# Two of the modulation's column blocks summed on VectorE instead of multiplied on TensorE

## The chip, the cores and the metric

The kernel runs on one core of a Trainium2 chip. The metric is the time of one execution in microseconds, taken on the device; for the kernel before the median of three runs is 1099.94 us. Beside the time there is one profile of one execution, with every instruction of every engine: TensorE (PE, and PEld for its weight loads), VectorE (DVE), ScalarE (ACT), GpSimd (POOL) and SyncE (SP), whose queue issues most of the DMAs of this kernel.

## The reference, cut to what matters

The program is one decoder layer on a sequence of 1024 tokens of width 1024 in float32. Ahead of everything stands a modulation: a vector c goes through silu and a 1024 x 6144 matrix, and its first two parts, shift and scale, change the normalised input. What the change touches is this:

```
c_act = jax.nn.silu(c)
mod = c_act @ w_ada[l] + b_ada[l]
sh1, sc1, g1, sh2, sc2, g2 = [m[:, None, :] for m in jnp.split(mod, N_MOD, axis=-1)]
h = rmsnorm(x, pre_w_mix[l]) * (1.0 + sc1) + sh1
proj = h @ w_in[l]
aq, ak, av, hq, hf, hi, hg = jnp.split(proj, _SPLITS, axis=-1)
```

Behind it follow windowed attention on aq, ak, av, a gated recurrence on the rest, an output projection, a second modulation and a squared-ReLU MLP. None of that is touched.

## The kernel before

**Tiles.** The 1024 columns of h are eight blocks of 128 (kb = 0 to 7), the tokens two halves of 512. For each block and half, x is transposed on TensorE (`first_T`), so that a column of h lies on a partition, and shift and scale of the block are one number per partition. `split_evac` (line 224) then makes two tiles of 128x512: ScalarE writes `hhi` (scaled and shifted, rounded to the matmul's type), GpSimd forms `f` from it, VectorE writes the rest, `hlo`. Each product with a weight is three passes on TensorE: high by high, high by low, low by high. The weights are split the same way: ScalarE copies the high part (`first_wq`, `first_kv`), VectorE subtracts to get the low part (`first_wql`, tiles `wq1l`, `wkv1l` and so on).

**The loop of the first stage** (lines 406 to 455) goes over kb for the first half of the tokens and adds into open PSUM banks for q (`pq`) and for k and v (`pk`). In one turn, TensorE does: the high products of block kb for four groups of 128 tokens (`first_mm(..., 0)`), the fold of a modulation if there is one, the transposes of x for block kb + 1, and the low products of block kb (`first_mm(kb, tb, 1)`). The evacuation of a block needs its shift (`sh1`), its scale (`a1`) and, on GpSimd, the negated shift (`ns1`). From line 336 to line 640 each of ScalarE, VectorE, GpSimd and TensorE executes in exactly the order in which the program is written (`pin`); behind line 640 the framework orders the instructions by a plan of its own.

**The modulation.** Shift and scale of blocks 0 and 1 come one block at a time. Blocks 2 and 3, 4 and 5, 6 and 7 come in pairs, as q = (1, 0), (2, 0), (3, 0). For a pair, eight tiles of weights (128x512 each, `wa`) hold the 1024 rows of c by 256 columns of shift (gate 0) and 256 of scale (gate 1), two blocks of rows side by side in a tile. `mod_mm` (line 281) multiplies them on TensorE: 16 products of 128x256 for the first half of kp and 16 for the second, with c spread over 32 columns as the stationary side, so that four sets run in four column groups. `mod_copy` brings the result to SBUF, and `mod_fold` turns it with two products against a constant, adds the bias on VectorE and writes `sh1`, `a1` and `ns1`. The table `nextq` says in which turn each pair is made: pair (2, 0) in turn kb = 3, its first reader being the evacuation of block 4, pair (3, 0) in turn kb = 5, for block 6.

**Loads.** SyncE's queue issues, in this order: x for the first half, `wa` of blocks 0 and 1, a first weight, `wa` of pair (1, 0), weights, `wa` of pair (2, 0), weights, `wa` of pair (3, 0), weights. Within a pair the tiles come as kp = 0, 1, 2, 3, each with gate 0 and then gate 1. In turn kb = 3 the loads of x for the second half are issued; ScalarE squares them in turns 5 and 6 (`norm_sq`, tiles `jx`), VectorE scales them in turns 6 and 7. The tiles `f`, `jx`, the copy of `mod_copy` and the sums of later modulations share one pool of five places (`t_`).

Later modulations (`modacc`, line 146) are already summed on VectorE, with tiles named `macc`; the later stage from 180 us on shows these operations.

Of the kernel before, what the change touches and what calls it, by code (L numbers as in the profile page):

```python
# [9 lines left out]
F32 = mybir.dt.float32  # L10
# [3 lines left out]
ALU = mybir.AluOpType  # L14
AX = mybir.AxisListType

P = 128
D = 1024
KB = D // P
# [28 lines left out]
def hybrid_layer(ctx: ExitStack, tc: tile.TileContext, I, out, dbg=None):  # L48
    nc = tc.nc
    ACT, DVE, POOL, PE, SP = (Queue(tc, e) for e in (nc.scalar, nc.vector, nc.gpsimd, nc.tensor, nc.sync))  # L50
# [17 lines left out]
    small = ctx.enter_context(tc.tile_pool(name="small", bufs=2, side="right"))  # L68
# [17 lines left out]
    def t_(name, shape=(P, 512), dt=F32):  # L86
        return T2.tile(list(shape), dt, tag="t2", name=name)
# [4 lines left out]
    def tp_ps(name):  # L92
        return pb.tile([P, 512], F32, tag="b", name=name)
# [21 lines left out]
    ident, cT, bT, prew1, prew2 = (tab[:, a:b] for a, b in ((0, P), (P, 136), (136, 184), (184, 192), (192, 200)))  # L115
# [10 lines left out]
    cs = tiny0.tile([P, KB], F32, tag="cs", name="cs")  # L126
# [3 lines left out]
    prew1s = small.tile([P, KB], F32, tag="prew1s", bufs=1, name="prew1s")  # L130
# [103 lines left out]
    def first_evac(th, kb, pst, then=None):  # L234
        hh[kb][th] = (hT_(f"hhi{kb}_{th}", F32R), hT_(f"hlo{kb}_{th}", F32R))
        c = slice(kb, kb + 1)
        split_evac(pst, a1[:, c], sh1[:, c], ns1[:, c], *hh[kb][th], f"f{th}_{kb}", then)
# [35 lines left out]
    sh1 = tiny0.tile([P, KB], F32, tag="sh1", name="sh1")  # L273
    ns1 = tiny1.tile([P, KB], F32, tag="ns1", name="ns1")
    a1 = tiny1.tile([P, KB], F32, tag="a1", name="a1")
# [16 lines left out]
    def mod_copy(q):  # L292
        n = 256 if q[0] else P
        pm[q, 0] = t_(f"ms{q[0]}_{q[1]}", (P, n))
        DVE.tensor_copy(pm[q, 0], pm[q][:, :n])

    def mod_fold(q):
        n = 2 if q[0] else 1
        pst, ms = pm[q], pm[q, 0]
        for j in range(n):  # L300
            PE.matmul(pst[:, 256 + P * j:256 + P * j + P], lhsT=ms[:, P * j:P * j + P], rhs=sel, start=True, stop=True)
        s2 = small.tile([P, 2], F32, tag="m1s", name=f"m1s{q[0]}_{q[1]}")
        cols = pst[:, 256:256 + n * P].rearrange("p (n g j) -> p g n j", g=2, j=64)[:, :, :, 0]
        c = slice(2 * q[0] + q[1], 2 * q[0] + q[1] + n)
        DVE.tensor_tensor(s2[:, :n], cols[:, 1], bT[:, 8 + c.start:8 + c.stop], ALU.add)
        DVE.tensor_tensor(sh1[:, c], cols[:, 0], bT[:, c], ALU.add)
        DVE.scalar_tensor_tensor(a1[:, c], s2[:, :n], 1.0, prew1s[:, c], ALU.add, ALU.mult)
        DVE.tensor_scalar(ns1[:, c], sh1[:, c], -1.0, None, ALU.mult)

    wa1, wqr, wkvr = {}, [], []  # L310

    def load_wa(q, kp, gate=0):
# [86 lines left out]
    def first_wql(kb):  # L399
        hi, lo = wq[kb]  # L400
        DVE.tensor_tensor(lo, wqr[kb], hi.bitcast(F32), ALU.subtract)

    first_wq(0)
    first_wql(0)
    nextq = {0: (0, 1), 1: (1, 0), 3: (2, 0), 5: (3, 0)}
    for kb in range(KB):
        q = nextq.get(kb)
        first_evac(0, kb, xT0[kb], None if kb else lambda: first_kv(0, DVE))
        if kb == 0:
            pq0 += [tp_ps("pq2"), tp_ps("pq3")]  # L410
            pks = [tp_ps("pk01"), tp_ps("pk23")]
            pk0 += [pks[tb // 2][:, tb % 2 * 256:tb % 2 * 256 + 256] for tb in range(4)]
            wkvr.append(load_raw(raw_, "wkvr3", I["w_kv"][3]))
        if kb + 1 < KB:
            first_wq(kb + 1)
        if kb == 3:
            norm_scale(0, 1, ACT)
            pin(True, SP)
            for hf in range(2):
                for tb in range(4, TB):  # L420
                    load_x(tb, (hf,))
            pin(False, SP)
        if kb and q:
            mod_mm(q, range(2))
        for which in ((0,), (1,)) if kb == 0 else ((0, 1),):
            first_mm(kb, 0, 0, which)
            first_mm(kb, 1, 0, which)
            if kb and q:
                mod_mm(q, range(2, 4))
                mod_copy(q)  # L430
            first_mm(kb, 2, 0, which)
            first_mm(kb, 3, 0, which)
            if kb == 0 and which[0] == 0:
                mod_mm(q)
                mod_copy(q)
        if kb + 1 < KB:
            first_wql(kb + 1)
        if q:
            mod_fold(q)
        if kb in (1, 3, 5):  # L440
            first_kv((kb + 1) // 2, DVE)
        if kb + 1 < KB:
            xT0.append(first_T(0, kb + 1))
        if kb in (5, 6):
            for tb in range(4, TB):
                norm_sq(tb, (kb - 5,))
        if kb == 6:
            norm_rstd(1, 0, 4)
            norm_scale(1, 0, DVE)
        if kb == 7:  # L450
            norm_scale(1, 1, DVE)
        if kb == KB - 1:
            xT1 = [first_T(1, 0), first_T(1, 1, a_ps)]
        for tb in range(4):
            first_mm(kb, tb, 1)
# [673 lines left out]
    wt, wh, araw = {}, {}, {}  # L1129
# [549 lines left out]
def layout(x, c, w_ada, b_ada, pre_w_mix, w_in, attn_sinks, attn_out_w, lb_table,  # L1679
           hg_norm_w, w_out, post_w_mix, pre_w_mlp, w_up, w_down, post_w_mlp):  # L1680
    A = {}
    f = lambda a: np.ascontiguousarray(a)
    cols = lambda v: f(np.asarray(v).reshape(-1, P).T)
    A["x"] = f(np.asarray(x)[0])
    t_cT = cols(np.asarray(c)[0])
    wa = np.asarray(w_ada)[0]
    w1 = wa[:, :2048]
    A["wada1"] = f(w1.reshape(4, 2, P, 2, 4, 256).transpose(3, 4, 0, 2, 1, 5).reshape(2, 4, 4, P, 512))
    A["wada1"][:, 0] = (w1.reshape(2, 2, 2, P, 2, 8, P)[:, :, :, :, :, :2].transpose(1, 5, 0, 3, 4, 2, 6)
                        .reshape(2, 4, P, 512))  # L1690
    A["wada"] = f(wa.reshape(KB, P, 6, 2, 512).transpose(2, 3, 0, 1, 4))
    ba = np.asarray(b_ada)[0]
    t_bT = cols(ba)
    A["b_g1"] = f(ba[2048:3072])
    A["b_g2"] = f(ba[5120:6144])
    t_prew1 = cols(np.asarray(pre_w_mix)[0])
    t_prew2 = cols(np.asarray(pre_w_mlp)[0])
    A["postw1"] = f(np.asarray(post_w_mix)[0])
    A["postw2"] = f(np.asarray(post_w_mlp)[0])
    wi = np.asarray(w_in)[0]  # L1700
    perm = [0, 4, 1, 5, 2, 6, 3, 7]
    A["w_q"] = f(wi[:, :512].reshape(D, 8, 64)[:, perm].reshape(KB, P, 512))
    A["w_kv"] = f(wi[:, 512:768].reshape(4, 2, P, 256).transpose(0, 2, 1, 3).reshape(4, P, 512))
    A["w_hv"] = f(wi[:, 1792:2304].reshape(KB, P, 512))
    hd = np.stack([wi[:, 1280:1792], wi[:, 768:1280], wi[:, 2304:2816]])
    A["w_hd"] = f(hd.reshape(3, KB, P, 4, P).transpose(3, 0, 2, 1, 4).reshape(4, 3, P, D))
    sk = np.asarray(attn_sinks)[0]
    order = [0, 1, 4, 5, 2, 3, 6, 7]
    A["sinks"] = f(np.broadcast_to(sk[order], (P, 8)))
    A["attw"] = f(np.asarray(attn_out_w)[0].reshape(8, 64)[perm].reshape(4, P).T)  # L1710
    A["lbt"] = f(np.asarray(lb_table).reshape(2, 4, P).transpose(2, 0, 1))
    A["hgw"] = f(np.asarray(hg_norm_w)[0].reshape(P, 1))
    wo = np.asarray(w_out)[0]
    A["w_o"] = f(np.concatenate([wo[:512].reshape(8, 64, D)[perm].reshape(4, P, D), wo[512:].reshape(4, P, D)]))
    A["w_u"] = f(np.asarray(w_up)[0].reshape(KB, P, 32, P).transpose(2, 1, 0, 3).reshape(32, P, D))
    A["w_dn"] = f(np.asarray(w_down)[0].reshape(32, P, D))
    A["tab"] = f(np.concatenate([np.eye(P, dtype=np.float32), t_cT, t_bT, t_prew1, t_prew2], 1))
    inv = (np.float64(500000.0) ** (-np.arange(0, 16, 2) / 16.0)).astype(np.float32)
    ang = (np.arange(1024, dtype=np.float32)[:, None] * inv[None, :]).astype(np.float64)
    co, si = np.cos(ang).astype(np.float32), np.sin(ang).astype(np.float32)  # L1720
    A["cosT"] = f(np.concatenate([co, co], 1).reshape(TB, P, 16).transpose(1, 0, 2))
    A["sinT"] = f(np.concatenate([-si, si], 1).reshape(TB, P, 16).transpose(1, 0, 2))
    i = np.arange(P)
    A["mle"] = (i[None, :] <= i[:, None]).astype(np.int32)
    A["fle"] = (i[:, None] <= i[None, :]).astype(np.float32)
    si_, ti = i[:, None], i[None, :]
    A["hmask"] = (si_ <= ti).astype(np.int32)
    A["rmask"] = f(np.broadcast_to((np.arange(512) % CH != 0).astype(np.float32), (P, 512)))
    return A
# [14 lines left out]
```

## Time and profile before

| what | value |
|---|---|
| median of three runs | 1099.94 us (1099.77 to 1101.99) |
| profiled execution: span, first to last instruction | 1097.6 us |
| profiled execution's own time | not told beside its span; the median of the runs is 2.3 us longer than the span |
| TensorE busy | 1076.2 us |
| VectorE busy | 795.1 us |
| ScalarE busy | 584.6 us |
| GpSimd busy | 373.2 us |
| granted TensorE clock, mean | 0.996 |
| `pm<-wa,csr` products of the three pairs | 96 of 128x256 |
| loads of `wa` | 32 of 256 KB |

A row of a timeline has the start in us, the length in us, engine, line, operation, output<-inputs, shapes and how many follow each other without a change; in brackets stands how long the engine was idle before and what ended that. Almost all instructions are issued through one helper and carry its line, L39, so one goes by the names of the tiles. A row of the view by stretches has start:end, the length, then for TensorE, its weight loads, VectorE, ScalarE and GpSimd the busy time and the number of instructions, then the granted clock, the DMAs' share and GB/s.

### The profile page before, as it was taken

What the parts mean: (1) busy time and instruction counts of PE and PEld (TensorE: products, weight loads), DVE (VectorE), ACT (ScalarE), POOL (GpSimd) and SP (SyncE); (2) the same over time, 40 slices, a digit from 0 to 9 for tenths busy, and PEclk for the clock granted to TensorE, in tenths of its full rate; (3) what the DMA queues carried; (4) which work ended last, traced back from release to release, by engine and by line L of the source; (5) the groups of instructions that cost most, each with busy time, mean ns of one, the idle gap of its engine ahead of it and who ended that gap; (6) DMA issues with size and microseconds to landing.
All of it is one profiled execution on the core that took longest, in us unless ns stands there. A gap on an engine that the chain in (4) does not pass through costs nothing.

```text
span 1097.6 us, 16208 instructions
## 1 busy us (share of the span) xinstructions
PE 1076.2 (98%) x5547; PEld 878.2 (80%) x5547; DVE 795.1 (72%) x1323; ACT 584.6 (53%) x1206; POOL 373.2 (34%) x499
## 2 busy tenths in 40 slices
PE   8999999999999999999999999999999999999995
PEld 6788776778888888888888888888888888888884
DVE  4365777878865574559776767876767787899876
ACT  3445544364565764566655555556664543555434
POOL 1153211033324663432543444533333333310014
PEclk9999999999999999999999999999999999999998
DMA  9701301534310352324577676767998888998537
GB/s 347 265 7 57 117 1 43 181 101 140 125 56 11 108 182 96 125 79 144 194 246 249 233 259 227 257 216 244 320 364 289 275 299 259 337 308 272 169 76 131
DMA packets 101587, 203.37 MB, mean 185 GB/s; under 512 B 13025, under 2 KB 13681, under 8 KB 101505
## 3 DMA queue, kind: packets, MB, share of 16 engines
q1 hardware_dynamic: 85968, 154.52, 41.4%
q0 software_dynamic: 15392, 47.57, 14.3%
q8 instruction: 43, 0.70, 0.3%
q14 instruction: 40, 0.32, 0.1%
q10 hardware_dynamic: 144, 0.26, 0.1%
HBM read 147.25 MB, written 55.05 MB: 184 GB/s over the span
## 4 chain that ended last, share of the span: by engine, by line
PE 92%; DVE 3%; ACT 1%; DMA 1%; POOL 1%; issue 1%; SPq 0%; DVEq 0%; POOLq 0%; ACTq 0%
PE pda L39 16%; PE pua L39 14%; PE pdc L39 8%; PE po L39 8%; PE puc L39 7%; PE pu L39 4%; PE pdb L39 4%; PE pq L39 4%; PE phg L39 4%; PE phq L39 3%; PE pub L39 3%; PE phf L39 3%; PE pv L39 3%; PE pk L39 2%; PE o L39 1%; PE sc L39 1%
## 5 line engine op out<-in xcount | busy, mean ns | idle before, releaser
L39 POOL TENSOR_TENSOR b<-b,b 128x512 f32<-128x512 f32 x64 | 89.6, 1400 | 222.8 <-DMA b<-w_dn 222.4
L39 ACT ACTIVATE dw<-dwr 128x512 fp32r<-128x512 f32 x72 | 45.4, 630 | 46.5 <-DMA dwr<-td 32.4
L39 ACT ACTIVATE s<-s 128x512 f32<-128x512 f32 x84 | 53.0, 631 | 31.8 <-DVE s L39 30.5
L39 DVE TENSOR_TENSOR dw<-dwr,dw 128x512 fp32r<-128x512 f32 x72 | 53.6, 744 | 9.0 <-ACT dw L39 8.9
L39 DVE TENSOR_TENSOR acc<-pda,acc 128x512 f32<-128x512 f32 x68 | 46.5, 684 | 13.7 <-PE pda L39 13.3
L39 POOL DMA_DIRECT2D td<-b x64 | 36.3, 567 | 21.6 <-POOL b L39 18.7
L39 POOL TENSOR_TENSOR rrf<-ssf,mhalf 128x1 f32<-128x1 f32 x7 | 7.9, 1253 | 95.3 <-DVE ssf L39 95.3
L39 DVE TENSOR_TENSOR wt<-s,wt 128x512 fp32r<-128x512 f32 x42 | 37.2, 886 | 2.6 <-ACT wt L39 2.5
L39 ACT ACTIVATE s<-pua 128x512 f32<-128x512 f32 x28 | 16.7, 598 | 39.4 <-PE pua L39 33.9
L39 ACT ACT_TABLE_LOAD x28 | 35.9, 1283 | 1.2 <-PEq L1737 0.7
L39 DVE SCALAR_TENSOR_TENSOR macc<-wada,cs,macc 128x512 f32<-128x512 f32 x42 | 33.7, 803 | 3.4 <-DMA wada<-wada 2.9
L39 POOL DMA_DIRECT2D b<-w_dn x64 | 34.4, 540 | 0.0
L39 POOL TENSOR_TENSOR comb<-comb,rd 128x512 f32<-128x512 f32 x8 | 11.7, 1458 | 63.3 <-DVE rd L39 44.2
L39 PE MATMUL pua<-bt_0h,wt 128*128 128x512 f32 x84 | 32.7, 389 | 0.0
L39 PE MATMUL pua<-bt_1h,wt 128*128 128x512 f32 x84 | 32.7, 389 | 0.0
L39 PE MATMUL pua<-bt_3h,wt 128*128 128x512 f32 x84 | 32.7, 389 | 0.0
L39 PE MATMUL pua<-bt_2h,wt 128*128 128x512 f32 x84 | 32.7, 389 | 0.0
L39 DVE TENSOR_TENSOR wt<-a,wt 128x512 fp32r<-128x512 f32 x42 | 31.0, 738 | 0.9 <-ACT wt L39 0.9
L39 DVE TENSOR_TENSOR acc<-pdc,acc 128x512 f32<-128x512 f32 x36 | 24.6, 684 | 8.5 <-PE pdc L39 8.4
L39 ACT ACTIVATE wt<-s 128x512 fp32r<-128x512 f32 x42 | 26.3, 626 | 8.2 <-DVE s L39 8.0
L39 PE MATMUL pda<-dw,du_6h 128*128 128x512 f32 x96 | 29.6, 389 | 0.0
L39 PE MATMUL pda<-dw,du_7h 128*128 128x512 f32 x96 | 29.5, 389 | 0.0
(757 smaller groups left out, 3746.1 us busy)
## 6 DMA issues: line engine op xcount, KB each, us to landing
dur<-ud SPq DMA_DIRECT2D x112, 256.0 KB, 4.5
wada<-wada SPq DMA_DIRECT2D x64, 256.0 KB, 3.5
b<-w_dn POOLq DMA_DIRECT2D x64, 256.0 KB, 5.2
td<-b POOLq DMA_DIRECT2D x64, 256.0 KB, 3.3
dwr<-td SPq DMA_DIRECT2D x64, 256.0 KB, 4.3
a<-w_u SPq DMA_DIRECT2D x56, 256.0 KB, 4.4
dwr<-w_dn SPq DMA_DIRECT2D x48, 256.0 KB, 4.5
ud<-s SPq DMA_DIRECT2D x42, 256.0 KB, 3.6
```

The costliest lines, as they stand in the source:

```text
L39: ins = op(*args, **kw)
```

## The change

Pairs (2, 0) and (3, 0) leave TensorE. The host fills their eight `wa` tiles in another way: tile k now holds one block of 128 rows of c, with the 256 columns of shift and the 256 of scale side by side. VectorE multiplies tile k by c's block k, one number per partition, and adds it to a tile `macc1` of 128x512: eight operations for a pair. Five of them stand at the end of turn 2 (or 4), three in turn 3 (or 5), behind the evacuation and ahead of the low part of the next weight. Then four transposes on TensorE bring the tile to PSUM, ahead of the transposes of x, one reduction on VectorE sums over the former partitions, and four small operations write `sh1`, `a1` and `ns1`. The products, the copy and the fold of these two pairs are gone. The order of the loads, and the tiles loaded, are the same.

```diff
         DVE.scalar_tensor_tensor(a1[:, c], s2[:, :n], 1.0, prew1s[:, c], ALU.add, ALU.mult)
+        DVE.tensor_scalar(ns1[:, c], sh1[:, c], -1.0, None, ALU.mult)
+
+    macc1 = {}
+
+    def mod_sum(q, ks):
+        for k in ks:
+            wt, c = wa1[q, k % 4, k // 4], cs[:, k:k + 1]
+            if k == 0:
+                macc1[q] = t_(f"macc1_{q[0]}")
+                DVE.tensor_scalar(macc1[q], wt, c, None, ALU.mult)
+            else:
+                DVE.scalar_tensor_tensor(macc1[q], wt, c, macc1[q], ALU.mult, ALU.add)
+
+    def mod_turn(q):
+        pst = a_ps(f"pmt{q[0]}")
+        for j in range(4):
+            PE.transpose(pst[:, j * P:(j + 1) * P], macc1[q][:, j * P:(j + 1) * P], ident)
+        red = small.tile([P, 4], F32, tag="mred", name=f"mred1_{q[0]}")
+        DVE.tensor_reduce(red, pst.rearrange("p (j k) -> p j k", j=4), AX.X, ALU.add)
+        c = slice(2 * q[0], 2 * q[0] + 2)
+        s2 = small.tile([P, 2], F32, tag="m1s", name=f"m1s{q[0]}")
+        DVE.tensor_tensor(s2, red[:, 2:4], bT[:, 8 + c.start:8 + c.stop], ALU.add)
+        DVE.tensor_tensor(sh1[:, c], red[:, 0:2], bT[:, c], ALU.add)
+        DVE.scalar_tensor_tensor(a1[:, c], s2, 1.0, prew1s[:, c], ALU.add, ALU.mult)
         DVE.tensor_scalar(ns1[:, c], sh1[:, c], -1.0, None, ALU.mult)
...
-    nextq = {0: (0, 1), 1: (1, 0), 3: (2, 0), 5: (3, 0)}
+    nextq = {0: (0, 1), 1: (1, 0)}
...
+        if kb in (3, 5):
+            mod_sum((kb // 2 + 1, 0), range(5, KB))
         if kb + 1 < KB:
             first_wql(kb + 1)
         if q:
             mod_fold(q)
+        if kb in (3, 5):
+            mod_turn((kb // 2 + 1, 0))
+        if kb in (2, 4):
+            mod_sum((kb // 2 + 1, 0), range(5))
         if kb in (1, 3, 5):
             first_kv((kb + 1) // 2, DVE)
...
+    A["wada1"][:, 2:] = (w1.reshape(2, 4, P, 2, 4, 256)[:, :, :, :, 2:].transpose(0, 4, 1, 2, 3, 5)
+                         .reshape(2, 2, 4, P, 512))
```

## Prediction

> **What bounds the kernel now.** I read the page first (busy shares, then the chain that ended last), then the stretches of the first stage one contraction block at a time, then the timelines of TensorE, VectorE, ScalarE and GpSimd in that stage.
>
> ```profile
> PE 1076.2 (98%) x5547; PEld 878.2 (80%) x5547; DVE 795.1 (72%) x1323; ACT 584.6 (53%) x1206; POOL 373.2 (34%) x499
> PE 92%; DVE 3%; ACT 1%; DMA 1%; POOL 1%; issue 1%; SPq 0%; DVEq 0%; POOLq 0%; ACTq 0%
> ```
>
> TensorE is busy for 98% of the span and carries 92% of the chain. So time taken from TensorE shortens the program, if nothing takes its place. The next view cuts the first stage into its blocks (start:end, length, then busy time and count of each engine, clock, DMA share, GB/s).
>
> ```profile
> 29.57:34.31 4.74, 4.74 (x31) 3.99 (x29) 1.35 (x2) 1.41 (x4) 0.73 (x2) 1.00 1.06 406
> 34.31:41.71 7.40, 7.40 (x65) 5.55 (x65) 2.81 (x8) 4.16 (x7) 0.59 (x2) 1.00 1.03 388
> 41.71:46.44 4.73, 4.73 (x31) 3.99 (x29) 1.35 (x2) 1.41 (x4) 0.86 (x2) 1.00 0.79 262
> 46.44:53.83 7.39, 7.39 (x65) 5.55 (x65) 2.81 (x8) 4.17 (x12) 0.53 (x2) 1.00 0.13 38
> 53.83:58.47 4.64, 4.64 (x31) 4.11 (x29) 2.65 (x8) 3.33 (x10) 1.77 (x3) 1.00 0.19 57
> ```
>
> These are kb = 2, 3, 4, 5, 6. TensorE (first pair) never idles. Blocks 3 and 5 hold the products that go, and last 7.4 us where a plain block lasts 4.64. VectorE (third pair) works 1.35 of 4.74 us in blocks 2 and 4, where five of the eight new sums go.
>
> **What goes from TensorE and what comes.** A pair of blocks takes 12.14 us (29.57 to 41.71) and 12.12 us (41.71 to 53.83); two plain blocks are 9.28. Sixteen products twice and a fold of four passes thus cost 2.86 and 2.84 us, hand-overs included.
>
> ```profile
> 29.57 0.40 PE L39 MATMUL pq<-wq2h,hhi 128*128 128x512 f32 x1
> 32.36 0.60 PE L39 MATMUL xT<-c_tab,x 128*128 128x128 f32 x4
> 34.31 1.07 PE L39 MATMUL pm<-wa,csr 128*32 128x256 f32 x16
> 39.42 0.61 PE L39 MATMUL pm<-sel,ms 128*128 128x128 f32 x4
> 39.86 0.60 PE L39 MATMUL xT<-c_tab,x 128*128 128x128 f32 x4
> ```
>
> In their place stand four transposes of 128x128 for each sum; the four passes of the fold have that shape and hold TensorE for 0.44 us (39.42 to 39.86). TensorE alone would gain 2.86 + 2.84 - 0.88 = 4.82 us. That is the most the change can bring.
>
> **What VectorE gets.** Each of the two column blocks needs one tensor_scalar and seven scalar_tensor_tensor over 128x512, each reading what the one before wrote, and one reduction from PSUM. A later stage has the same operations.
>
> ```profile
> 195.18 0.48 DVE L39 TENSOR_SCALAR macc<-wada,cs 128x512 f32<-128x512 f32 x1
> 195.69 0.75 DVE L39 SCALAR_TENSOR_TENSOR macc<-wada,cs,macc 128x512 f32<-128x512 f32 x1
> 211.31 3.11 DVE L39 SCALAR_TENSOR_TENSOR macc<-wada,cs,macc 128x512 f32<-128x512 f32 x4
> 274.33 1.76 DVE L39 SCALAR_TENSOR_TENSOR macc<-wada,cs,macc 128x512 f32<-128x512 f32 x2
> 274.50 1.05 POOL L39 TENSOR_SCALAR k<-f 128x512 f32<-128x512 f32 x1 [3.63 <-DVE f L39]
> L39 DVE TENSOR_REDUCE mred<-pmod x4: 677/677/678, 288.7 to 349.8; 128x4 f32<-128x512 f32 x4
> ```
>
> The first operation is followed 0.51 us later by the next (195.18 to 195.69). Four dependent sums in a row took 3.11 us: one every (3.11 - 0.75) / 3 = 0.79 us. Two that ran beside a GpSimd tensor_scalar took 1.76, against 0.79 + 0.75 = 1.54, and that GpSimd operation took 1.05. So where they meet, I add 0.22 us to VectorE and take 1.05 for GpSimd. The reduction is 0.68.
>
> At this point a rule speaks against the change. The Trainium skill (Vector Engine (DVE) Microarchitecture Reference, Points that are easy to get wrong) says that the scalar_tensor_tensor form with two non-bf16 SBUF sources halves throughput. By that rule the sums would be far longer, and the time that of the fourth rival below. The trace doesn't bear it out: macc has both sources in SBUF as f32 and took 0.75 (195.69), and hlo, with one of its sources in PSUM, takes the same 0.75 (34.67 below).
>
> **Block 3 step by step.** The order on VectorE is written out: wq3l, five sums, hlo of block 3, three sums, wq4l, reduction and four small operations, wkv2l.
>
> ```profile
> 30.63 0.68 DVE L39 TENSOR_TENSOR wq3l<-wqr,wq3h 128x512 fp32r<-128x512 f32 x1
> 33.00 0.78 ACT L39 ACTIVATE hhi<-xT,sh,a 128x512 fp32r<-128x512 f32 x1 [3.33 <-PE xT L39]
> 33.94 0.69 POOL L39 TENSOR_SCALAR f<-hhi,ns 128x512 f32<-128x512 f32 x1 [4.01 <-ACT hhi L39]
> 34.67 0.75 DVE L39 SCALAR_TENSOR_TENSOR hlo<-xT,a,f 128x512 fp32r<-128x512 f32 x1 [3.35 <-POOL f L39]
> 40.06 0.16 DVE L39 TENSOR_TENSOR m1s<-pm,c_tab 128x2 f32<-128x2 f32 x1 [1.01 <-PE pm L39]
> 40.51 0.78 ACT L39 ACTIVATE hhi<-xT,sh,a 128x512 fp32r<-128x512 f32 x1 [3.24 <-DVE ns L39]
> 42.17 0.75 DVE L39 SCALAR_TENSOR_TENSOR hlo<-xT,a,f 128x512 fp32r<-128x512 f32 x1 [1.08 <-POOL f L39]
> 42.84 0.68 DVE L39 TENSOR_TENSOR wq5l<-wqr,wq5h 128x512 fp32r<-128x512 f32 x1
> 15.08 0.78 ACT L39 ACTIVATE hhi<-xT,sh,a 128x512 fp32r<-128x512 f32 x1 [0.97 <-DVE ns L39]
> 15.91 0.50 PE L39 MATMUL pq<-wq0h,hhi 128*128 128x512 f32 x1 [0.38 <-ACT hhi L39]
> ```
>
> VectorE sat idle for 3.35 us ahead of hlo; the sums fill that hole. An independent operation starts 0.08 us before the end of the one in front (42.17 + 0.75 against 42.84). So the sums begin at 31.23, the second at 31.74, the fifth at 34.11, which ends at 34.85. GpSimd's f starts at 33.94 in the middle of that: f until 34.99, sums until 35.07. Either way hlo starts at 35.02, 0.35 late. The last three sums start at 35.69 (0.67 after hlo), 36.48 and 37.27, and end at 38.01.
>
> TensorE is earlier than that. Its block 3 starts at 34.21 (34.31 less the 0.10 by which block 2 is longer than 4.64), the first part lasts 2.79 us (29.57 to 32.36), and at 37.00 it stands before the transposes and waits until 38.04 (0.03 hand-over, as between the fold's end at 40.03 and 40.06). Queued behind them are the transposes of x for block 4 and the low products of block 3; ScalarE's hhi, GpSimd's f and VectorE wait on these. A new wait of 1.04 us.
>
> From there: transposes out after 0.60 (38.64), reduction 38.67 to 39.35, hhi of block 4 at 39.80 (40.06 to 40.51 is 0.45), block 4 on TensorE 0.83 later (15.08 to 15.91), at 40.63. TensorE's own work would be done at 38.04 + 0.44 + 0.44 + 1.41 = 40.33 (the low products are 4.64 - 2.79 - 0.44): a second wait of 0.30. Block 4 starts at 40.63 instead of 41.71: of 2.42 us, 1.08 is left. The 0.60 us of wq4l lies beside the transposes and costs nothing; without them it would cost its 0.60.
>
> **Blocks 4 and 5.** hhi 39.80, f 0.94 later (33.00 to 33.94) at 40.74, hlo 0.73 later at 41.47, wq5l 42.14, sums from 42.74, the fifth ends at 46.36, or 46.58 with f beside it; f itself runs from 45.00 (x transposed from 43.42, hhi 0.64 later, f 0.94 later) to 46.05. hlo starts at 46.50, the three sums end at 49.49. TensorE gets there at 40.63 + 4.64 + 2.79 = 48.06 and waits 1.46 us. Block 6 follows 2.59 us after 49.52, as before (38.04 to 40.63): at 52.11 instead of 53.83. **Sum: 1.72 us earlier**; the four waits eat 3.1 of the 4.82.
>
> **What else is touched.** No DMA moves: the same tiles in the same order, only the host fills them otherwise.
>
> ```profile
> 19.90 5.60 SPq L39 DMA_DIRECT2D wa<-wada  x8
> 27.74 4.87 SPq L39 DMA_DIRECT2D wa<-wada  x8
> DMA to landing us min/median/max: 5.0/5.2/6.0
> 57.76 2.03 DVE L39 TENSOR_SCALAR x<-x,r_x 128x512 f32<-128x512 f32 x4 [1.13 <-POOL r_x L39]
> 61.25 1.04 PE L39 MATMUL xT<-c_tab,x 128*128 128x128 f32 x8
> ```
>
> The eight tiles are issued by 25.5 and 32.6 and land within 6.0 us, by 31.5 and 38.6. The fourth sum, which takes the seventh tile of the queue, starts at 33.32 and 44.83, so no sum waits for a load. The scaled x for the second half ends at 59.79 and is needed at 61.25. Its chain starts at hhi of block 6, which moves 0.37 us closer to TensorE (39.80 to 40.63 is 0.83, before it was 40.51 to 41.71, 1.20): 1.1 us of slack is left, cost nothing. If that slack were gone, each 0.1 us late would be 0.1 us of TensorE. Behind that, TensorE carries the chain and the 1.72 us go through. The program behind is ordered by the framework, not by hand; I allow 0.4 us either way, a fifth of the 2.13 us in which TensorE idles between 61.2 and 130:
>
> ```profile
> 61.20:72.00 10.80, 10.31 (x62) 8.10 (x61) 7.14 (x13) 6.76 (x10) 5.47 (x8) 1.00 0.01 2
> 72.00:100.00 28.00, 27.88 (x198) 24.51 (x198) 16.03 (x53) 11.10 (x33) 15.18 (x44) 1.00 0.06 20
> 100.00:130.00 30.00, 28.48 (x191) 20.82 (x190) 22.91 (x52) 18.96 (x73) 7.91 (x14) 1.00 0.44 141
> ```
>
> The profiled execution has a span of 1097.6 us, 2.3 less than the median of the runs, 1099.94. The span becomes 1095.9; I take the same distance around it: **1098.2 us**.
>
> **Rivals.** First, the sums are quicker: no meeting with GpSimd, and one every 0.67 us, as independent operations follow each other (42.17 to 42.84). Then hlo stays at 34.67, the sums end at 37.42, block 4 starts at 40.04, block 6 at 50.71: 3.12 us earlier, 1096.8. For it speaks that the hole on VectorE is just long enough; against it the row of four. With 0.79 us but without GpSimd's part both blocks save 0.2 more: 1097.7, which I count to the forecast.
>
> Second, a tile wait takes the gain. The sum's tile comes from a pool of five that also serves f and the squares of x on ScalarE. It is held until the transposes of block 5, about 50.1. If the first of four squares got that place, they would run after it:
>
> ```profile
> 46.86 0.61 ACT L39 ACTIVATE jx<-x 128x512 f32<-128x512 f32 x1
> 49.22 0.19 ACT L39 ACTIVATION_READ_ACCUMULATOR jx<-x 128x1 f32 x1
> ```
>
> Their 2.55 us (46.86 to 49.41) put hhi of block 6 at 52.65 and block 6 at 53.48: 0.35 us gained, 1099.6. Against it: with places taken in turn, it is the fourth square that meets the held one, and that has time (50.1 + 0.8 before 51.28).
>
> Third, slower: the sums run long on VectorE, as in this row.
>
> ```profile
> 247.38 3.23 DVE L39 SCALAR_TENSOR_TENSOR macc<-wada,cs,macc 128x512 f32<-128x512 f32 x3
> 250.53 0.53 DVE L39 TENSOR_SCALAR f<-f,omlb,lb 128x512 f32<-128x512 f32 x1
> ```
>
> That is 3.15 / 3 = 1.05 us each. All 14 sums lie on the path, so 14 x 0.26 = 3.6, less the 0.44 already counted, turns 1.72 gained into 1.5 lost: 1101.4. It decides from 0.94 us each (14 x 0.154 = 2.16). Against it: GpSimd works 0.53 to 0.86 us a block here.
>
> Fourth, all sums at double length, if two f32 sources in SBUF halved the rate: 14 x 0.75 = 10.5, less 0.44 and 1.72, is 8.3 us lost, 1108.3. The row of 0.75 us speaks against it. This is what the rule of the Trainium skill above would give.
>
> **How the numbers follow.** Forecast 0.52, quick sums 0.26, tile wait 0.10, long sums 0.10, doubled 0.02. A measurement of this kernel can tell about 0.2% from no change, 2.2 us: 1097.74 to 1102.14. Faster than that: nearly all of the quick sums (0.25) and 0.08 of the forecast, 0.33. Slower: the doubled case and 0.07 of the long sums (beyond 1.09 us each), 0.09. The rest, 0.58, is within. The range goes from 1096.4 (quick sums and the 0.4 us behind) to 1101.0 (it takes in the tile wait and sums of up to 1.02 us each) and leaves out under 2 in 10. The likeliest case alone: 1097.7 (no meeting with GpSimd) to 1098.6 (the 0.4 us behind).
>
> **What would show it.** Right: four waits of TensorE, for the sums about 1.0 and 1.5 us in blocks 3 and 5, and 0.3 each at the start of blocks 4 and 6; sums one every 0.79 us; f at 1.05 us beside them; block 6 near 52.1. Wrong: TensorE without a wait for the sums (gain towards 4.8), ScalarE waiting at the squares, sums of 0.94 us or more, or block 6 early by 1.7 us and the gain given back behind 61 us.

## The result, and the profile after

The changed kernel takes 1097.86 us, median of 17 runs (1097.15 to 1101.11); the kernel before, in 17 runs beside it, 1100.14 us. The ratio is 0.998, with a 95% interval of 0.9973 to 0.9987: 2.28 us less, just at the 2.2 us that the prediction called the limit of what can be told from no change. The forecast of 1098.2 is 0.34 us off.

From here on, stretches are counted from the start of block 2, the last place that the change can't have moved: the profiled execution of the changed kernel was the longest of its 17 (1101.11 us, span 1099.3). In it x landed 0.37 us later, TensorE's granted clock was 0.66 from 10 to 14 us (1.00 in the kernel before), and TensorE was 1.95 us late at block 2, ahead of every changed instruction.

The page of the changed kernel: busy times, and the chain that ended last.

```profile
PE 1074.6 (98%) x5483; PEld 877.0 (80%) x5483; DVE 802.8 (73%) x1339; ACT 583.6 (53%) x1206; POOL 373.1 (34%) x499
PE 83%; DMA 7%; DVE 5%; ACT 2%; issue 1%; POOL 1%; SPq 0%; DVEq 0%; POOLq 0%; ACTq 0%
```

TensorE works 1.6 us less, with 64 records less (3.9 less in blocks 3 and 5, by the stretches below; ahead of block 2, with the lower clock, it worked 27.45 us instead of 26.19, and behind block 6 another 1.1 us longer); VectorE works 7.7 us more. The chain now leaves TensorE in more places. The stretches of blocks 2 to 6 in the same execution (start:end, length, then busy time and count of TensorE, its weight loads, VectorE, ScalarE, GpSimd; clock, DMA share, GB/s):

```profile
31.52:36.17 4.65, 4.65 (x31) 4.10 (x29) 4.10 (x7) 1.32 (x4) 0.72 (x2) 1.00 1.06 404
36.17:42.79 6.62, 5.45 (x35) 4.45 (x33) 6.12 (x12) 3.89 (x8) 0.43 (x1) 1.00 1.05 400
42.79:47.53 4.74, 4.74 (x28) 4.21 (x29) 3.81 (x6) 1.67 (x4) 0.95 (x2) 1.00 0.65 190
47.53:54.48 6.95, 5.46 (x34) 4.45 (x33) 6.42 (x13) 3.90 (x12) 0.76 (x1) 1.00 0.00 0
```

Blocks 3 and 5 lost 1.95 and 1.93 us of TensorE's work (7.40 and 7.39 busy before, 5.45 and 5.46 now), but got only 0.78 and 0.44 us shorter. VectorE now works 6.12 of 6.62 us and 6.42 of 6.95 there. What holds TensorE up is in its timeline:

```profile
31.52 0.40 PE L39 MATMUL pq<-wq2h,hhi 128*128 128x512 f32 x1
40.08 0.66 PE L39 MATMUL pmt<-c_tab,macc 128*128 128x128 f32 x4 [0.97 <-DVE macc L39]
40.58 0.60 PE L39 MATMUL xT<-c_tab,x 128*128 128x128 f32 x4
42.79 0.50 PE L39 MATMUL pq<-wq4h,hhi 128*128 128x512 f32 x1 [0.20 <-ACT hhi L39]
51.78 0.66 PE L39 MATMUL pmt<-c_tab,macc 128*128 128x128 f32 x4 [1.29 <-DVE macc L39]
54.48 0.50 PE L39 MATMUL pq<-wq6h,hhi 128*128 128x512 f32 x1 [0.20 <-ACT hhi L39]
```

Four waits, at the four places predicted. Block 2 to block 4 takes 11.27 us (12.14 before), block 4 to block 6 11.69 (12.12 before). The stage is 1.30 us shorter, not 1.72, and not 4.82. In the time, 2.28 us came out. Another 1 us has to be found elsewhere. Setting the starts of all matmuls side by side, the changed kernel (in its second profile, below, which has no late start) keeps its distance to the kernel before from block 6 to the end within 0.3 us, but for one place, where it wins 1.1 more. Before:

```profile
215.20 0.75 DVE L39 SCALAR_TENSOR_TENSOR macc<-wada,cs,macc 128x512 f32<-128x512 f32 x1 [0.78 <-DMA wada<-wada]
217.24 0.75 DVE L39 SCALAR_TENSOR_TENSOR macc<-wada,cs,macc 128x512 f32<-128x512 f32 x1 [1.28 <-DMA wada<-wada]
227.63 0.50 PE L39 MATMUL phg<-hhi,whg0h 128*128 128x512 f32 x1 [1.28 <-ACT f L39]
```

And the changed kernel:

```profile
215.74 0.75 DVE L39 SCALAR_TENSOR_TENSOR macc<-wada,cs,macc 128x512 f32<-128x512 f32 x1 [0.40 <-DMA wada<-wada]
217.27 0.75 DVE L39 SCALAR_TENSOR_TENSOR macc<-wada,cs,macc 128x512 f32<-128x512 f32 x1 [0.78 <-DMA wada<-wada]
227.66 0.50 PE L39 MATMUL phg<-hhi,whg0h 128*128 128x512 f32 x1 [0.38 <-ACT f L39]
```

In a later modulation that the change doesn't touch, two sums wait for loads, 2.06 us before and 1.18 after, and TensorE's wait behind them goes from 1.28 to 0.38. On each engine the instructions come in the same order in both kernels but for the edit, and the loads are issued in the same order. So there were two questions for the chip: do the sums alone set the four waits in the stage, and why does a load at 212 us land sooner?

### The profile page after: what moved, and what is told of

It reads as the page before. It is cut to its first block, busy times and chain, and to the rows that moved or that the text cites. A ratio compares the mean times of both kernels' runs of the same rounds, so it can differ in the third digit from the quotient of the medians.

```text
span 1099.3 us, 16110 instructions
## 1 busy us (share of the span) xinstructions
PE 1074.6 (98%) x5483; PEld 877.0 (80%) x5483; DVE 802.8 (73%) x1339; ACT 583.6 (53%) x1206; POOL 373.1 (34%) x499
## 4 chain that ended last, share of the span: by engine, by line
PE 83%; DMA 7%; DVE 5%; ACT 2%; issue 1%; POOL 1%; SPq 0%; DVEq 0%; POOLq 0%; ACTq 0%
PE pda L39 14%; PE pua L39 13%; PE pdc L39 7%; PE po L39 7%; PE puc L39 6%; PE pu L39 4%; PE pdb L39 4%; PE phg L39 4%; PE phq L39 3%; PE phf L39 3%; PE pub L39 3%; PE pv L39 3%; PE pq L39 2%; DMA wa<-wada 1%; DMA dwr<-td 1%
## 5 line engine op out<-in xcount | busy, mean ns | idle before, releaser
L39 DVE TENSOR_TENSOR wt<-s,wt 128x512 fp32r<-128x512 f32 x42 | 33.8, 805 | 2.6 <-ACT wt L39 2.5
L39 DVE TENSOR_TENSOR s<-puc,s 128x512 f32<-128x512 f32 x14 | 9.7, 690 | 28.5 <-issue 26.0
```

The costliest lines, as they stand in the source:

```text
L39: ins = op(*args, **kw)
```

## The experiments

**The two kernels once more, for a second profile of each.** No edit.

> The changed kernel itself, once more, for a second profile. In its first profile TensorE reached block 2 at 31.52 us instead of 29.57, by a later start of the program ahead of every changed instruction. Both theories expect block 2 near 29.6 here, blocks 2 and 3 together 11.3 us and blocks 4 and 5 together 11.7 us (12.1 and 12.1 before the change), so block 6 near 52.5 instead of 53.83. They part behind it. Theory (the gain of the first stage goes through to the end, with about 1 us more from the wait at 220 to 230 us): TensorE idles less than 1.3 us between 220 and 230. Rival (a load that lands at a fixed time holds the program at 217 us): it idles about 2.5 us there.

> The kernel before once more, for a second profile. Theory and rival expect the same stretches as in the first: block 2 at 29.6, block 4 at 41.7, block 6 at 53.8, and a wait of TensorE between 220 and 230 us. If that wait is again 1.3 us it belongs to the program; if it is well below 1 us, it comes and goes with the loads, and nothing can be read from it about the change.

The changed kernel, one run, took 1098.02 us with a span of 1095.8, the kernel before 1099.92. TensorE in the changed kernel:

```profile
29.34 0.40 PE L39 MATMUL pq<-wq2h,hhi 128*128 128x512 f32 x1
40.59 0.50 PE L39 MATMUL pq<-wq4h,hhi 128*128 128x512 f32 x1 [0.20 <-ACT hhi L39]
52.30 0.50 PE L39 MATMUL pq<-wq6h,hhi 128*128 128x512 f32 x1 [0.20 <-ACT hhi L39]
225.29 0.50 PE L39 MATMUL phg<-hhi,whg0h 128*128 128x512 f32 x1 [0.16 <-ACT f L39]
```

With a start like that of before (29.34 against 29.57) the stretches are 11.25 and 11.71 us, as in the first profile, and block 6 is 1.53 us earlier, 0.23 of it from the start. TensorE's wait for f is 0.16; in the second profile of the kernel before it was 1.14. So both findings repeat.

**Two sums of eight left out.** The sums of tiles 6 and 7 are dropped in both pairs; shift and scale of column blocks 4 to 7 lack these terms.

```diff
-            mod_sum((kb // 2 + 1, 0), range(5, KB))
+            mod_sum((kb // 2 + 1, 0), range(5, 6))
```

> The last two of the eight sums of each pair are left out (so shift and scale of blocks 4 to 7 lack a quarter of their terms); all else as in the changed kernel. Theory (VectorE's dependent sums, each 0.79 us, set when TensorE goes on): the sums end 1.57 us earlier, the waits of 0.97 and 1.29 us ahead of the transposes vanish, the waits of 0.2 us for the next block's evacuation stay; blocks 2 and 3 take 10.3 us, blocks 4 and 5 take 10.4, and the time falls by 2.3 us to about 1095.6. Rival one (TensorE's own order, the transposes ahead of the transposes of x and the low products, costs the time): waits and time stay, 1097.9. Rival two (a load at 217 us holds the program): the stretches shorten, the time stays at 1097.9 and the wait of TensorE at 220 to 230 us grows by 2.3.

1099.15 us, ratio to before 0.9991 (0.9982 to 1.0): slower than the changed kernel, where about 1095.6 was expected: a miss. The waits ahead of the sum's transposes are gone and block 4 to block 6 takes 10.19 us instead of 11.69, but block 3 has a new wait, and ScalarE says for what:

```profile
36.08 0.78 ACT L39 ACTIVATE hhi<-xT,sh,a 128x512 fp32r<-128x512 f32 x1 [5.74 <-DMA wa<-wada]
36.91 0.50 PE L39 MATMUL pq<-wq3h,hhi 128*128 128x512 f32 x1 [2.13 <-ACT hhi L39]
```

The high half of a block, which reads no `wa`, waits for a load of `wa`: with its readers gone, presumably the load itself stands between that tile's place and its next user. The experiment thus took work away and added a wait; it shows the step for blocks 4 to 6 and nothing on the total. The next one mends that.

**Two sums of eight made narrow.** All tiles keep their readers, but tiles 6 and 7 are summed over 8 of 512 columns.

```diff
-                DVE.scalar_tensor_tensor(macc1[q], wt, c, macc1[q], ALU.mult, ALU.add)
+                n = 8 if k > 5 else 512
+                DVE.scalar_tensor_tensor(macc1[q][:, :n], wt[:, :n], c, macc1[q][:, :n], ALU.mult, ALU.add)
```

> The changed kernel, but the sums of the tiles k = 6 and 7 of both pairs take 8 columns of 512 (every tile still has its reader, so that no buffer changes hands at another place); shift and scale of column blocks 4 to 7 lack most of those tiles' terms. If TensorE's waits in blocks 3 and 5 are nothing but the sums on VectorE, they end 1.2 to 1.5 us earlier in each block: the waits ahead of the transposes of the sum (0.97 and 1.29 us in the changed kernel) and the two of 0.20 ahead of the high products all fall below 0.1, block 2 to block 4 takes 10.2 to 10.4 us instead of 11.27, block 4 to block 6 10.2 to 10.5 instead of 11.69, and the time is 2.2 to 2.6 us less than the changed kernel's: 1095.3 to 1095.7. If something else stands just behind them (f on GpSimd, the loads of the weights, ScalarE's high half), a wait of 0.5 us or more for that shows in the same places, the stretches stay above 10.9, and the time stays above 1096.5.

1095.88 us (ratio 0.9966, 0.9953 to 0.9978), 1.98 us below the changed kernel. TensorE, with block 2 at 30.04:

```profile
40.25 0.50 PE L39 MATMUL pq<-wq4h,hhi 128*128 128x512 f32 x1 [0.21 <-ACT hhi L39]
48.20 0.66 PE L39 MATMUL pmt<-c_tab,macc 128*128 128x128 f32 x4 [0.26 <-DVE macc L39]
50.90 0.50 PE L39 MATMUL pq<-wq6h,hhi 128*128 128x512 f32 x1 [0.20 <-ACT hhi L39]
```

The stretches are 10.21 and 10.65 us, and no other wait stepped in. Less went than I expected, because the three last sums still took 1.26 us instead of 2.31: 1.05 us less for each pair, not 1.2 to 1.5. So the waits of 1.29 and 0.20 became 0.26 and 0.20.

**TensorE's other work ahead of the sum's transposes.** In turns 3 and 5 the transposes of x and half of the low products come before the transposes of the sum.

```diff
+            xT0.append(first_T(0, kb + 1))
+            for tb in range(2):
+                first_mm(kb, tb, 1)
...
-        if kb + 1 < KB:
+        if kb + 1 < KB and kb not in (3, 5):
...
-        for tb in range(4):
+        for tb in range(2 if kb in (3, 5) else 0, 4):
```

> The changed kernel, but in blocks 3 and 5 TensorE does the transposes of the next x block and half of the low products (two of four row blocks) ahead of the transposes of the sum, instead of behind them; VectorE's order is the same. If VectorE's chain (sums, reduce, shift and scale, and then ScalarE's high half) sets when the next block begins, the waits ahead of the transposes fall from 0.97 and 1.29 us to under 0.3, but the ones ahead of the high products of blocks 4 and 6 grow from 0.20 to about 1.0 and 1.3, the stretches stay at 11.1 to 11.3 and 11.5 to 11.7, and the time stays within 0.5 us of the changed kernel's 1097.9. If the waits cost time only because of the place where TensorE meets them, the stretches fall to 10.4 and 10.6 and the time to 1095.7.

1097.75 us (0.9984, 0.9976 to 0.9993), with block 2 at 29.63:

```profile
38.22 0.61 PE L39 MATMUL pmt<-c_tab,macc 128*128 128x128 f32 x4
40.87 0.50 PE L39 MATMUL pq<-wq4h,hhi 128*128 128x512 f32 x1 [1.34 <-ACT hhi L39]
52.56 0.50 PE L39 MATMUL pq<-wq6h,hhi 128*128 128x512 f32 x1 [1.34 <-ACT hhi L39]
```

The waits ahead of the transposes are gone, and the one ahead of the high products of the next block has grown to 1.34. The stretches are 11.24 and 11.69 us: unchanged. Filling TensorE's hole gains nothing; the chain through VectorE sets when the next block begins.

**The sums spread over earlier turns.** Two of the eight go one turn further ahead, five into the turn before, and only one stays behind the evacuation. The terms are the same, added in another order.

```diff
-            mod_sum((kb // 2 + 1, 0), range(5, KB))
+            mod_sum((kb // 2 + 1, 0), (7,))
...
-            mod_sum((kb // 2 + 1, 0), range(5))
+            mod_sum((kb // 2 + 1, 0), (1, 5, 2, 6, 3))
+        if kb in (1, 3):
+            mod_sum(((kb + 3) // 2, 0), (0, 4))
```

> All eight sums, but in three places instead of two: two at the end of the turn before, five where five are now, one where three are now, in the order in which the tiles are loaded. Theory: the sums end ahead of TensorE's 37.0 and 48 us, both waits ahead of the transposes vanish as in the kernel with two sums left out, blocks 2 and 3 take 10.3 us and blocks 4 and 5 about 10.4; time about 1095.6. If the two early sums meet a load that has not landed (the tiles of the first pair are issued from 19.9 us and land 5 to 6 us later; the first sum would start at 28.9) the gain of the first pair is lost in part. Rival one: time and waits as in the changed kernel, 1097.9. Rival two: stretches shorter, time 1097.9.

1096.12 us (0.9963, 0.9949 to 0.9977), the fastest kernel here that leaves nothing out: 1.74 us below the changed one. TensorE, with block 2 at 29.83:

```profile
40.25 0.50 PE L39 MATMUL pq<-wq4h,hhi 128*128 128x512 f32 x1 [0.20 <-ACT hhi L39]
48.28 0.66 PE L39 MATMUL pmt<-c_tab,macc 128*128 128x128 f32 x4 [0.33 <-DVE macc L39]
50.98 0.50 PE L39 MATMUL pq<-wq6h,hhi 128*128 128x512 f32 x1 [0.20 <-ACT hhi L39]
```

The stretches are 10.42 and 10.73, together 1.8 us shorter for the same 16 operations, since fewer of them stand between the evacuation and the transposes. The time of 1095.6 that I expected wasn't reached: of the wait in block 5, which should have vanished, 0.33 us is left.

**Where do TensorE's instructions come from?** Now the second gain. The trace has a DMA queue (q8) whose packets are of the kind "instruction", 43 of 16 KB in the changed kernel. It has 5483 matmul records and as many weight loads, 10966 in all, or 255 for each packet. (A second queue of that kind, q14 with packets of 8 KB, has none from 28 us before to 16 us behind the issue of the loads at 212 us, in any profile.) In the kernel before, one packet starts in the middle of the three loads of wada issued at 212 us; in the changed kernel none does, and the change took 64 matmul records and 64 weight loads, half a packet, from TensorE ahead of it. The first trial to move the packets added 64 products of 32x32x128 to the changed kernel, ahead of the transposes of the sum, and 69 in place of 5 of the first 15 to the kernel before, in its wait for x. Either was meant to add 128 instructions, half a packet:

```diff
+        for i in range(28 if q[0] == 2 else 36):
+            PE.matmul(pst[32 * (i % 4):32 * (i % 4) + 32, 0:32], lhsT=csr[:, 0, :], rhs=ident[:, 0:32], start=True, stop=True,
+                      tile_position=(0, 32 * (i % 4)))
```

```diff
-    idle(15)
+    idle(10)
+    for i in range(69):
+        PE.matmul(spare_ps[32 * (i % 4):32 * (i % 4) + 32, 0:32], lhsT=ones[:, 0:32], rhs=ones[:, 0:32], start=True, stop=True,
+                  tile_position=(0, 32 * (i % 4)))
```

> [...] The computation is the changed kernel's. If the second gain (TensorE's wait for f at 220 to 230 us, 1.1 to 1.3 us before and 0.2 to 0.4 after) comes from the packet of 16 KB of TensorE's instructions no longer lying among the loads of wada at 211 to 217 us, then that packet is back between 211 and 215 us, VectorE's sums at 215 to 218 us wait for wada 1.7 us or more in all, TensorE's wait for f is 1.0 us or more, and the time is 0.7 to 1.0 us above the changed kernel's: 1098.6 to 1098.9, with the stretches of blocks 2 to 6 unchanged within 0.2. If the gain there is the stage's own shift in time, or chance, the wait stays at 0.2 to 0.4 and the time at 1097.9 (up to 1098.2 if the added products overrun the waits).

> [...] If the packet of TensorE's instructions among the loads of wada costs the kernel before 0.8 us, that packet moves about 10 us away from 212 to 215 us, TensorE's wait for f at 220 to 230 us falls from 1.1 to 1.3 us to 0.2 to 0.5, and the time falls by 0.6 to 1.0 us against the kernel before: 1099.1 to 1099.5, unless the packet meets another load elsewhere. If the gain at 220 us belongs to the changed stage, the wait stays above 1.0 and the time within 0.3 of the kernel before.

1097.80 us (0.9983, 0.9974 to 0.9992) and 1099.95 us (1.0001, 0.9992 to 1.001). Taken as they were meant, both miss. But the traces show each such product as two records: I had added a whole packet, not half of one, and the packets lie where they were in both (202.5 us in the first, 213.3 in the second; a 44th is behind them). For the changed kernel this is then a control: 128 records more, no packet among the loads, no loss in the median, though TensorE's wait for f was 0.69 us in its profile. The kernel before kept its packet, yet TensorE waited only 0.34 us for f; its start was 0.81 us later at block 2, which ate the gain. The packet there started 0.3 us behind SyncE's issue, for the most part ahead of the loads' own packets.

**Half a packet.** The same with 32 products, which are 64 records and 64 weight loads. In the changed kernel they are 14 and 18 in place of 28 and 36; in the kernel before, 32 stand in its wait for x:

```diff
-        for i in range(28 if q[0] == 2 else 36):
+        for i in range(14 if q[0] == 2 else 18):
```

```diff
     idle(15)
+    for i in range(32):
+        PE.matmul(spare_ps[32 * (i % 4):32 * (i % 4) + 32, 0:32], lhsT=ones[:, 0:32], rhs=ones[:, 0:32], start=True, stop=True,
+                  tile_position=(0, 32 * (i % 4)))
```

> As padded_tensor, but with 14 and 18 added products: the trace of padded_tensor shows each such product as two records (56 for 28), so that its 64 products were 256 instructions with their weight loads, a whole packet, and left the packets where they were (202.5 us, beside 202.2 in the changed kernel). 32 products are 64 records and 128 instructions, what the change took away. The computation is the changed kernel's. If the packet of TensorE's instructions costs the time at 220 us, one packet starts 0.5 to 3 us behind SP's issue of the last three loads of wada (211 to 214 us), the last sum that needs them begins 4.8 to 5.2 us behind that issue (3.8 to 4.3 in the changed kernel), TensorE's wait for f is 0.9 us or more, and the time is 0.7 to 1.0 us above the changed kernel's: 1098.6 to 1098.9. If the packet has no part in it, the last sum begins 3.6 to 4.6 us behind the issue, the wait is 0.2 to 0.7, and the time 1097.7 to 1098.1.

> The kernel before, with 32 products of 32 by 32 by 128 added behind the first 15 that keep TensorE busy, in its wait of 1.2 us for x: 64 records of 0.01 us, 128 instructions. The computation is the same, and block 2 begins within 0.3 us of the kernel before. If the packet of TensorE's instructions costs the time at 220 us, the packet at 213.0 to 214.7 us lies at about 202 us or 224 us instead, the last sum that needs wada begins 3.6 to 4.3 us behind SP's issue of the last three loads (5.0 and 5.2 in the two profiles of the kernel before), TensorE's wait for f is 0.1 to 0.5 us, and the time falls by 0.7 to 1.0 us, to 1098.8 to 1099.1 where the kernel before has 1099.8. If the packet has no part in it, that wait stays at 1.1 us or more in an execution that starts like the kernel before's, and the time within 0.3 of it.

> The kernel before, unchanged, for a third profile of 200 to 230 us. If the packet costs the time there, it starts 0.5 to 3 us behind SP's issue of the last three loads of wada, the last sum begins 4.8 us or more behind that issue and TensorE's wait for f is 0.9 us or more, as in the other two; if the size of that wait is chance, this profile may show 0.2 to 0.5.

The padded changed kernel takes 1099.12 us (0.9991, 0.9982 to 1.0), the shifted kernel before 1098.90 (0.9989, 0.998 to 0.9997), where the kernel before has 1100.02 (21 runs); its third profile is of a run of 1099.54. The padded one loses 1.26 us against the changed kernel (0.7 to 1.0 expected), the shifted one gains 1.12. In the padded kernel, the DMA view of the 5 us from SyncE's issue on (210.8 to 215.8; the last number of an issue is its time to landing), then the two rows that depend on it:

```profile
q8 instruction: 1, 0.02, 1.1%
issues: line engine op xcount, KB each, median us to landing
wada<-wada SPq DMA_DIRECT2D x3, 256.0 KB, 4.1
```

```profile
215.94 0.75 DVE L39 SCALAR_TENSOR_TENSOR macc<-wada,cs,macc 128x512 f32<-128x512 f32 x1 [1.24 <-DMA wada<-wada]
226.32 0.50 PE L39 MATMUL phg<-hhi,whg0h 128*128 128x512 f32 x1 [1.23 <-ACT f L39]
```

The changed kernel, second profile, the same 5 us (210.85 to 215.85), has no line of q8:

```profile
q1 hardware_dynamic: 599, 1.08, 69.7%
wada<-wada SPq DMA_DIRECT2D x3, 256.0 KB, 2.9
```

These two executions begin alike (x at 8.59 and 8.61 us) and have the same block 6 (52.29 and 52.30). TensorE is at the same place in both until it waits for f, and 1.03 us later in the padded one from there on. The shifted kernel before (212.5 to 217.5, again without q8):

```profile
q1 hardware_dynamic: 613, 1.10, 71.9%
wada<-wada SPq DMA_DIRECT2D x3, 256.0 KB, 2.8
```

```profile
216.30 0.75 DVE L39 SCALAR_TENSOR_TENSOR macc<-wada,cs,macc 128x512 f32<-128x512 f32 x1 [0.43 <-DMA wada<-wada]
226.92 0.50 PE L39 MATMUL phg<-hhi,whg0h 128*128 128x512 f32 x1 [0.16 <-ACT f L39]
```

All profiles together; the third column counts from SyncE's issue of the three loads to the start of the nearest packet in the trace's records.

| kernel | median, us | packet | loads land after (median of three) | TensorE's wait for f |
|---|---|---|---|---|
| before, three profiles | 1099.80 to 1100.14 | +2.6, +1.0, +2.4 | 4.1, 4.0, 4.0 | 1.28, 1.14, 1.12 |
| changed, padded by half a packet | 1099.12 | +2.5 | 4.1 | 1.23 |
| before, shifted by a whole packet | 1099.95 | +0.3 | 3.1 | 0.34 |
| before, shifted by half a packet | 1098.90 | -8.7 | 2.8 | 0.16 |
| changed, two profiles | 1097.86 | -8.6, -8.6 | 3.3, 2.9 | 0.38, 0.16 |
| changed, padded by a whole packet | 1097.80 | -8.5 | 3.6 | 0.69 |
| low products first | 1097.75 | -10.8 | 2.8 | 0.16 |
| sums spread | 1096.12 | -9.4 | 2.7 | 0.16 |
| two sums narrow | 1095.88 | -9.3 | 3.2 | 0.16 |
| two sums left out | 1099.15 | -9.0 | 2.8 | 0.31 |

Wherever a packet starts 1.0 to 2.6 us behind the issue, the loads take 4.0 us or more; elsewhere 2.7 to 3.6. The traces also show a late end. The packet in the padded kernel took 0.88 us (the 1.1% above, of 5 us on 16 DMA engines). The load that SyncE issues behind the three, `whq1r`, landed after 4.3 us there and after 3.3 in the changed kernel's second profile. And from 215.8 to 217.2 us the padded kernel still has 11 DMA packets of 2 KB, of which the last nine start 0.08 us apart, the length of one, and 8 of under 512 B; the other has 2, both under 512 B. That fits one of the 16 engines ending its share later than the rest, but the trace doesn't name the engine of a packet.

## Why the prediction was right, and where it was not

The number and the range were right, the mechanism of the stage was right, but two terms were off in opposite directions: 0.42 us too much in the stage, and about 1 us missing behind it. That the time is only 0.34 us off is partly luck: 2.28 us were gained where 1.72 were forecast, and the kernel before came out 0.20 us above the 1099.94 from which the forecast was taken.

**TensorE's own gain and its four waits.** Right. The waits for the sums were predicted as 1.04 and 1.46 us and are 0.97 and 1.29; those ahead of blocks 4 and 6 were 0.30 each and are 0.20. That VectorE's chain sets the stage is shown from both sides: less work on it ahead of the transposes shortens the stretches (sums narrow or spread), another order on TensorE doesn't (low products first).

**VectorE's terms.** The order fits, and up to the transposes the places fit to 0.1 us; what was mis-sized shows in these rows of the changed kernel (VectorE, then ScalarE's and GpSimd's rows, each from its own timeline, then the view of the sums by operation with shortest, median and longest duration):

```profile
33.71 3.42 DVE L39 SCALAR_TENSOR_TENSOR macc<-wa,cs,macc 128x512 f32<-128x512 f32 x4
37.06 0.74 DVE L39 SCALAR_TENSOR_TENSOR hlo<-xT,a,f 128x512 fp32r<-128x512 f32 x1
37.72 2.31 DVE L39 SCALAR_TENSOR_TENSOR macc<-wa,cs,macc 128x512 f32<-128x512 f32 x3
40.78 0.69 DVE L39 TENSOR_REDUCE mred<-pmt 128x4 f32<-128x512 f32 x1
41.96 0.78 ACT L39 ACTIVATE hhi<-xT,sh,a 128x512 fp32r<-128x512 f32 x1 [2.73 <-DVE ns L39]
35.82 0.77 POOL L39 TENSOR_SCALAR f<-hhi,ns 128x512 f32<-128x512 f32 x1 [3.93 <-ACT hhi L39]
47.27 1.02 POOL L39 TENSOR_SCALAR f<-hhi,ns 128x512 f32<-128x512 f32 x1 [3.69 <-ACT hhi L39]
L39 DVE SCALAR_TENSOR_TENSOR macc<-wa,cs,macc x14: 735/752/1062, 33.7 to 51.0; 128x512 f32<-128x512 f32 x14
```

Four sums with f beside them took 3.42 us; I had 3.11 + 0.22 = 3.33: 0.09 short. The longest of the 14 took 1.06 us, the median 0.75. From the transposes' start to the reduction it is 0.70, not 0.63 (+0.07), and from the reduction to ScalarE's high half 1.18, not 1.13 (+0.05). That is 0.21 us for each pair and 0.42 for two: the stage gains 1.30 instead of 1.72. From the high half to TensorE's next block it is 0.83 (41.96 to 42.79), as predicted. GpSimd's f took 0.77 and 1.02 where I had 1.05 twice; VectorE was held up all the same.

**The loads in the stage.** Right: no sum of the stage waits for a `wa` tile. **The slack of the second half's x.** Right: in the first profile the changed kernel is 1.95 us behind at block 2, 0.65 at block 6 and 0.85 at 133 us, so what the stage won is kept to 0.2 us.

**"Behind that, TensorE carries the chain and the 1.72 us go through"**, with 0.4 us either way: this step failed. Some 0.9 us more came at 220 us, more than twice the allowance. I had asked which waits and DMAs the change moves, and found none; it moves the packets in which TensorE's own instructions arrive, by taking 128 of them away. Shown is that half a packet more brings the wait back in the changed kernel (1.23 us) and that half a packet more removes it from the kernel before (0.16). A whole packet more leaves both times as they were, with waits of 0.69 and 0.34. In the half-packet pairs the loads land 1.2 to 1.3 us earlier when no packet starts among them. How one packet of 16 KB delays three loads of 256 KB by that much isn't shown: that it stands in the way of theirs on one of the DMA engines is a reading, which the late single packets support. Nor is the scatter of 2.7 to 3.6 us without a packet explained.

By medians, the stage alone is worth 0.90 us (padded by half a packet: 1100.02 to 1099.12) and the packet alone 1.12 (before, shifted by half); together 2.02 of the 2.28. By the profiles it is 1.30 and 1.03. The intervals of the two ratios are each wide enough for either, and that of the padded kernel reaches 1.0; the profiles carry the split.

**The rivals.** Quick sums: wrong, the pitch is (2.31 - 0.75) / 2 = 0.78 and f does meet them. The tile wait: wrong; ScalarE's four squares run from 48.05 to 50.60 without one, beside sums that end at 51.72. Long sums: wrong as a mechanism for all 14, though the longest one has about that length (1.06). Doubled sums: wrong. The Trainium skill (Vector Engine (DVE) Microarchitecture Reference, Points that are easy to get wrong) says that this form with two non-bf16 SBUF sources halves throughput; the row above, 14 sums with both tensors in SBUF as f32 and a median of 0.752 us, disagrees with it, since `hlo`, with one source in PSUM, takes 0.74.

## What to carry to other kernels

When work moves to an engine with idle time, lay its instructions one by one into that engine's hole. Take the pitch of dependent operations, and the longer row for the one that meets a neighbour. Here that told the four waits to within 0.2 us each, and a gain in the stage of 1.72 us where 1.30 came out, when TensorE's own work alone would have promised 4.82. What is left then is to put more of the moved work ahead of the last step that the first engine waits for; reordering the waiting engine gained nothing. And a difference of about 0.1% between two kernels with different numbers of instructions can come from where the instruction packets fall: before crediting an edit with it, shift the count by half a packet in both.

## What the runs showed of the hardware that was not expected

TensorE's instructions come by DMA, about 255 to a packet of 16 KB, and one packet that starts 1.0 to 2.6 us behind the issue of three loads of 256 KB goes with a landing after 4.0 to 4.1 us instead of 2.7 to 3.6. In this program over 1 us hangs on it: 32 tiny products that compute nothing make the kernel before 1.12 us faster (ratio 0.9989, 0.998 to 0.9997).

A product of 32x32x128 in f32 is two records on TensorE, each with its own weight load. In the changed kernel padded by half a packet, 64 such records shorten TensorE's two waits by 0.82 us together, from 0.96 and 1.29 to 0.58 and 0.85.
